# Attention outputs split at the end of their value products and kept in DRAM as two halves, in a hybrid attention and convolution trunk

## The chip, the cores and the metric

The kernel runs on one core of a Trainium2 chip. The metric is the device time of one execution in microseconds (us): the median of three runs of the kernel before is 903.31 us (902.05 to 904.63). The engines are TensorE (PE, its weight loads PEld), VectorE (DVE), ScalarE (ACT), GpSimd (POOL) and SyncE (SP), which issues most DMAs. Each engine takes its own instructions strictly in its order and waits where an operand is not there.

## The reference

1024 tokens of width 1024 pass two layers, each a pre-RMSNorm, a mixer and a residual; a last RMSNorm follows. All is float32. Layer 0 is latent attention with 8 heads, layer 1 a gated Conformer convolution. What the change touches is the end of the attention:

```
s = where(mask, (q @ k.T) * scale, -inf)       # causal, 8 heads, q and k 128 + 64 wide
p = softmax(s)
o = p @ v                                      # 128 wide for each head
out = (concat_heads(o) * silu(gate)) @ w_out   # 1024 x 1024
```

## The kernel before

Float32 products are made of three matmuls of halves: a value x is kept as a high half (x rounded to the matmul's type, a ScalarE copy) and a low half (x minus the high half, a VectorE subtraction), and `mm3` (lines 137 to 140) adds high x high, high x low and low x high in PSUM. Activations lie transposed, channels on the 128 partitions and tokens along the row; a chunk c is 512 of the 1024 tokens.

The attention runs over the heads h = 0 to 7. For head h, `score(h, i)` makes the scores S_i of the 128 queries of block i (five matmuls for each 512 keys, PSUM tile S, two buffers), adds the mask, takes the maximum (VectorE), the exponential (ScalarE, which frees the S buffer) and scales the probabilities P_i (GpSimd). `attend(h, c)` transposes the probabilities of four blocks piece by piece (T, TensorE), evacuates each piece as a high half pth (ScalarE, line 594) and a low half ptl (VectorE, line 595), each from a ring of four SBUF buffers, and adds the value products po (`mm3`). At its end the gating, line 599, writes og. For 15 of the 16 attends og is stored in DRAM as it is (`ogS`, line 602), 14 times on SyncE's queue and for (7,1) on GpSimd's. The attend (7,0) splits its og directly into the tiles of the output projection (`split_og`, lines 617 and 618).

attend(h,0) is called after S_5 of head h, attend(h,1) after S_1 of head h+1. `proj(h+1)`, which makes the next head's queries and keys (pj, qh, ql, kh, kl) and for every second head the values (pv, vh, vl), is called after S_3 of head h, `split_early` after S_6 and others. The calls do not set the final order: a scheduler puts each engine's instructions in an order when the kernel is built, and buffers that are reused carry waits. In what follows (h,c) is an attend, and the end of an attend is the place of its last value matmul.

`load_og` (lines 620 to 624) brings an og back: one load into the low half's place, then a ScalarE copy into the high half and a VectorE subtraction. The seven of chunk 0 are loaded while head 7 is at work, the eight of chunk 1 in the output projection, `o_tile`, whose weights are loaded (wr_o) and split as they are needed, from the same queue.

Of the kernel before, what the change touches and what calls it, by code (L numbers as in the profile page):

```python
# [9 lines left out]
F32 = mybir.dt.float32  # L10
F32R = mybir.dt.float32r
# [7 lines left out]
P = 128  # L19
# [3 lines left out]
NH = 8  # L23
CK = 31
NTAP = 16
CH = 512
# [38 lines left out]
def hybrid_body(ctx, tc, xT, xP, pos, cols, w1a, w1b, wqr, wqk, wv, wo, wc, we, out):  # L65
    nc = tc.nc
    v, s, g, pe, sp = nc.vector, nc.scalar, nc.gpsimd, nc.tensor, nc.sync
# [23 lines left out]
    ropeS = [[tc.dram_tile([P, T], F32, name=f"ropeS{k}{p_}") for p_ in range(2)]  # L91
             for k in range(4)]
    gateS = [tc.dram_tile([P, T], F32, name=f"gateS{h}") for h in range(NH)]
    ogS = [[tc.dram_tile([P, CH], F32, name=f"ogS{h}{c}") for c in range(2)] for h in range(NH)]

    early_eng = [v]

# [39 lines left out]
    def mm3(ps, wh, wl, xh, xl, start, stop):  # L137
        pe.matmul(ps, wh, xh, start=start, stop=False)  # L138
        pe.matmul(ps, wh, xl, start=False, stop=False)  # L139
        pe.matmul(ps, wl, xh, start=False, stop=stop)  # L140
# [64 lines left out]
    def halves(ap):  # L205
        return ap.rearrange("p (b n) -> p b n", b=2)

    def sl(k, n=P):
        return slice(k * n, (k + 1) * n)
# [56 lines left out]
    def load_a(k, many):  # L266


        raw = wp.tile([P, 1024], F32, tag="wraw", name=f"wr_a{k}")
        hi = wp.tile([P, 1024], F32R, tag="w", bufs=5, name=f"wh_a{k}")  # L270
        lo = wp.tile([P, 1024], F32R, tag="w", bufs=5, name=f"wl_a{k}")
        n = 384 * many
        sp.dma_start(raw[:, :n], w1a[:, 384 * k : 384 * k + n])
        if k == 0:
            v.tensor_copy(hi[:, :n], raw[:, :n])
        else:
            s.activation(hi[:, :n], raw[:, :n], AF.Copy)
        r3, h3, l3 = (t_[:, :n].rearrange("p (a n) -> p a n", n=384) for t_ in (raw, hi, lo))
        v.tensor_tensor(h3[:, :, 320:], r3[:, :, 320:], h3[:, :, 320:].bitcast(F32), ALU.subtract)
        v.tensor_tensor(l3[:, :, :256], r3[:, :, :256], h3[:, :, :256].bitcast(F32), ALU.subtract)  # L280
        return hi, lo

    for k in range(KD):
# [4 lines left out]
        if k == 0 or k % 2 == 1:  # L288
            first, many = k, 1 if k in (0, KD - 1) else 2
            pair = load_a(k, many)  # L290
# [196 lines left out]
    b1 = es_b.enter_context(tc.tile_pool(name="b1", bufs=1, reuse_waits="tile"))  # L487
# [92 lines left out]
    def attend(h, c, dst=None):  # L580
        vh, vl = vpair[h // 2]
        vs = sl(h % 2)
        gt = heads[h][5]
        po = psA_p.tile([P, CH], F32, tag="acc", name=f"po{h}{c}")
        nj = 4 * (c + 1)
        for j in range(nj):
            il0 = max(0, j - 4 * c)
            pt = psT_p.tile([P, CH], F32, tag="T", name=f"T{h}{c}{j}")
            for il in range(il0, 4):
                pe.transpose(pt[:, sl(il)], probs[h, 4 * c + il][:, sl(j)], ident)  # L590
            hi = b1.tile([P, CH], F32R, tag="pth", bufs=4, name=f"pth{h}{c}{j}")
            lo = b1.tile([P, CH], F32R, tag="ptl", bufs=4, name=f"ptl{h}{c}{j}")
            n0 = il0 * P
            s.activation(hi[:, n0:], pt[:, n0:], AF.Copy)  # L594
            v.tensor_tensor(lo[:, n0:], pt[:, n0:], hi[:, n0:].bitcast(F32), ALU.subtract)  # L595
            mm3(po[:, n0:], vh[:, j, vs], vl[:, j, vs], hi[:, n0:], lo[:, n0:],
                j == 0, j == nj - 1)
        og = b1.tile([P, CH], F32, tag="og", bufs=2, name=f"og{h}{c}")
        v.tensor_tensor(halves(og), po.rearrange("p (n b) -> p b n", b=2),
                        gt[:, sl(c, CH)].rearrange("p (n b) -> p b n", b=2), ALU.mult)  # L600
        if dst is None:
            (g if (h, c) == (NH - 1, 1) else sp).dma_start(ogS[h][c], og)
        else:
            split_og(og, dst)

    def act_tile(grp, nm):
        if grp == "A":
            both = long_tile([P, 2, CH], F32R, f"a_{nm}")
        elif grp == "B":
            both = mix_tile([P, 2, CH], F32R, f"a_{nm}")  # L610
        else:
            both = act.tile([P, 2, CH], F32R, tag="act", name=f"a_{nm}")
        return both[:, 0, :], both[:, 1, :]

    def split_og(raw, pair):
        hi, lo = pair
        s.activation(hi, raw, AF.Copy)
        v.tensor_tensor(lo, raw, hi.bitcast(F32), ALU.subtract)

    def load_og(grp, h, c):  # L620
        pair = act_tile(grp, f"og{c}{h}")
        sp.dma_start(pair[1].bitcast(F32), ogS[h][c])
        split_og(pair[1].bitcast(F32), pair)
        return pair

    ogt = {}
# [2 lines left out]
    for h in range(NH):  # L629
        for i in range(8):  # L630
            score(h, i)
            if i == 1 and pending is not None:
                attend(*pending)
                pending = None
            if i == 3 and h + 1 < NH:
                proj(h + 1)
            if i == 4 and h < 2:
                split_early(wc[22 + h], f"cg{6 + h}")
            if i == 6:
                split_early(we[h], f"e{h}")  # L640
            if i == 5:
                if h < NH - 1:
                    attend(h, 0)
                else:
                    ogt[0] = [load_og("A", h_, 0) for h_ in range(NH - 1)]
                    ogt[0].append(act_tile("A", f"og0{h}"))
                    attend(h, 0, ogt[0][h])
        pending = (h, 1)
# [95 lines left out]
    def pk_tile(nm):  # L744
        return dp.tile([P, CH], F32, tag="pk", bufs=3, name=nm)

    ogt[1] = [load_og("B", h, 1) for h in range(NH)]

    ctx.enter_context(tc.manual_schedule(engines={mybir.EngineType.PE}))
# [411 lines left out]
```

## Time and profile before

| | us |
|---|---|
| runs, median (range) | 903.31 (902.05 to 904.63) |
| the profiled execution, its own time | 903.44 |
| its span | 901.7 |
| attention, from about 180 to 452: length | 272.00 |
| output projection, from about 452 to 524: length | 72.00 |

The profiled execution's time is 1.7 us longer than its span, which begins with the first and ends with the last instruction. The mean granted TensorE clock is 0.996 of full speed. In a row of the timeline the first number is the start in us from the span's start, the second the duration; a bracket says how long the engine sat idle before the row and what ended that. A matmul's duration includes the time that it takes to pass the pipeline, so that successive starts, not durations, tell the pace.

### The profile page before, as it was taken

To read this page: it belongs to the slowest core of one execution; us is meant where nothing else is said; L and a number is where in the kernel's file an instruction comes from. 1 tells how busy PE (TensorE), PEld (TensorE's weight loads), DVE (VectorE), ACT (ScalarE), POOL (GpSimd) and SP (SyncE) were. 2 spreads that over 40 slices of the span, in tenths; PEclk is the share of its full clock that TensorE was granted. 3 is DMA by queue.
4 is the path that set the end of the run, shared out by engine and by line. 5 is a ranking of instruction groups with operands and counts; after the bars stand their busy time and mean duration, and the time that the engine had idled before them with its cause. 6 is when DMAs were issued, how large, how long until landed. Compare 5 with 4: busy or idle time off the path is not lost.

```text
span 901.7 us, 12318 instructions
## 1 busy us (share of the span) xinstructions
PE 888.1 (98%) x4408; PEld 739.4 (82%) x4408; DVE 656.6 (73%) x1123; ACT 503.1 (56%) x838; POOL 346.9 (38%) x296
## 2 busy tenths in 40 slices
PE   9999999999999999999999999999999999999996
PEld 7888887888988988988788888888888887878996
DVE  7688857556656566686465868999999998687544
ACT  8535355255655554574444457766566773678732
POOL 0000000142532421642212259999999993000034
PEclk9999999999999999999999999999999999999998
DMA  7325635572422331651274411111113223136714
GB/s 270 117 71 171 230 131 188 193 228 85 141 92 81 121 116 40 219 178 33 77 264 125 163 48 54 47 51 38 47 48 110 95 80 113 50 138 196 259 61 144
DMA packets 39836, 110.69 MB, mean 123 GB/s; under 512 B 5280, under 2 KB 8352, under 8 KB 39776
## 3 DMA queue, kind: packets, MB, share of 16 engines
q1 hardware_dynamic: 39408, 109.27, 36.5%
q8 instruction: 34, 0.56, 0.3%
q10 hardware_dynamic: 288, 0.39, 0.1%
q14 instruction: 26, 0.21, 0.1%
q0 software_dynamic: 80, 0.26, 0.1%
HBM read 83.93 MB, written 24.92 MB: 121 GB/s over the span
## 4 chain that ended last, share of the span: by engine, by line
PE 69%; POOL 15%; issue 6%; DVE 5%; ACT 2%; DMA 2%; SPq 0%; POOLq 0%; DVEq 0%; ACTq 0%
POOL dcv L850 13%; PE ps_b L138 5%; PE ps_b L140 5%; PE ps_b L139 5%; PE T L590 3%; PE o L139 3%; PE o L140 3%; PE o L138 3%; PE e L138 3%; PE e L140 3%; PE e L139 3%; PE po L139 2%; PE S L564 2%; PE S L567 2%; PE po L140 2%
## 5 line engine op out<-in xcount | busy, mean ns | idle before, releaser
L850 POOL TENSOR_TENSOR dcv<-dcv,pkb 128x512 f32<-128x512 f32 (+1 forms) x126 | 159.2, 1266 | 7.5
L849 ACT ACTIVATE pkb<-u,taps 128x512 f32<-128x512 f32 (+1 forms) x126 | 83.9, 674 | 56.8 <-POOL dcv L850 53.6
L577 POOL TENSOR_SCALAR P<-P,st 128x128 f32<-128x128 f32 (+3 forms) x64 | 47.7, 747 | 125.9 <-DVE st L576 124.1
L861 DVE SCALAR_TENSOR_TENSOR av<-u,taps,av 128x512 f32<-128x512 f32 (+1 forms) x135 | 91.6, 688 | 1.6 <-ACT av L855 1.5
L863 DVE SCALAR_TENSOR_TENSOR cv<-su,gsum,cv 128x512 f32<-128x512 f32 (+1 forms) x117 | 80.6, 689 | 0.5
L107 POOL TENSOR_TENSOR wl_qk<-wr_qk,wh_qk 128x640 fp32r<-128x640 f32 x8 | 12.6, 1571 | 170.4 <-DMA ropeS<-rh 164.3
L594 ACT ACTIVATE pth<-T 128x512 fp32r<-128x512 f32 (+1 forms) x96 | 46.0, 491 | 55.3 <-PE T L590 54.2
L138 PE MATMUL ps_b<-xgh,wh_b 128*128 128x512 f32 x176 | 69.9, 397 | 0.0
L140 PE MATMUL ps_b<-xgh,wl_b 128*128 128x512 f32 x176 | 69.6, 395 | 0.0
L139 PE MATMUL ps_b<-xgl,wh_b 128*128 128x512 f32 x176 | 69.6, 395 | 0.0
L595 DVE TENSOR_TENSOR ptl<-T,pth 128x512 fp32r<-128x512 f32 (+1 forms) x96 | 52.0, 552 | 22.2 <-ACT pth L594 22.0
L1040 POOL TENSOR_TENSOR x<-x,rbe 128x512 f32<-128x512 f32 (+1 forms) x16 | 16.2, 1046 | 125.3 <-DMA rbe<-rowe 120.1
L138 PE MATMUL e<-a_y,wh_e 128*128 128x256 f32 (+1 forms) x192 | 61.7, 322 | 0.0
L140 PE MATMUL e<-a_y,wl_e 128*128 128x256 f32 (+1 forms) x192 | 61.5, 320 | 0.0
L139 PE MATMUL e<-a_y,wh_e 128*128 128x256 f32 (+1 forms) x192 | 61.4, 320 | 0.0
L574 ACT ACTIVATE P<-S,st 128x128 f32<-128x128 f32 (+3 forms) x64 | 47.4, 742 | 23.3 <-DVE st L572 18.4
L138 PE MATMUL cg<-a_h,wh_cg 128*128 128x512 f32 x128 | 51.7, 404 | 0.0
L138 PE MATMUL o<-a_og,wh_o 128*128 128x512 f32 x128 | 50.9, 399 | 0.0
L140 PE MATMUL o<-a_og,wl_o 128*128 128x512 f32 x128 | 50.9, 397 | 0.0
L138 PE MATMUL cb<-a_h,wh_cb 128*128 128x512 f32 x128 | 50.8, 397 | 0.0
L138 PE MATMUL ca<-a_h,wh_ca 128*128 128x512 f32 x128 | 50.8, 397 | 0.0
L572 DVE TENSOR_REDUCE st<-S 128x1 f32<-128x128 f32 (+3 forms) x64 | 48.3, 754 | 3.5
(321 smaller groups left out, 2625.0 us busy)
## 6 DMA issues: line engine op xcount, KB each, us to landing
wr_o<-in_wo_dram SPq DMA_DIRECT2D x16, 512.0 KB, 4.4
wr_e<-in_we_dram SPq DMA_DIRECT2D x14, 512.0 KB, 4.4
wl_e<-loSe SPq DMA_DIRECT2D x14, 512.0 KB, 4.1
wr_b<-in_w1b_dram SPq DMA_DIRECT2D x11, 512.0 KB, 4.1
sr_cg<-in_wc_dram SPq DMA_DIRECT2D x8, 512.0 KB, 4.2
loScg<-sl_cg SPq DMA_DIRECT2D x8, 512.0 KB, 2.9
gateS<-gt SPq DMA_DIRECT2D x8, 512.0 KB, 4.5
rq<-ropeS SPq DMA_DIRECT2D x32, 128.0 KB, 2.8
```

The costliest lines, as they stand in the source:

```text
L138: pe.matmul(ps, wh, xh, start=start, stop=False)
L139: pe.matmul(ps, wh, xl, start=False, stop=False)
L140: pe.matmul(ps, wl, xh, start=False, stop=stop)
L572: v.tensor_reduce(st[:, 0:1], ps[:, off : off + nk], AX.X, ALU.max, negate=True)
L574: s.activation(pr[:, :nk], ps[:, off : off + nk], AF.Exp, bias=st[:, 0:1], accum_out=st[:, 1:2])
L577: g.tensor_scalar(pr[:, :nk], pr[:, :nk], st[:, 2:3], 1.0, ALU.mult, ALU.mult)
L594: s.activation(hi[:, n0:], pt[:, n0:], AF.Copy)
L595: v.tensor_tensor(lo[:, n0:], pt[:, n0:], hi[:, n0:].bitcast(F32), ALU.subtract)
L849: s.activation(pk, lag(src, i), AF.Copy, scale=tap(of, i))
L850: g.tensor_tensor(acc, acc, pk, ALU.add)
L861: v.scalar_tensor_tensor(a_, lag(E, i), tap(dwe, i), a_, ALU.mult, ALU.add)
L863: v.scalar_tensor_tensor(c_, lag(su, i), tap(gsum, i), c_, ALU.mult, ALU.add)
```

## The change

`attend` splits og where it makes it, into two tiles that it takes from the rings pth and ptl (four buffers each), and stores both in two DRAM tiles. `load_og` loads both halves and splits nothing. 15 ScalarE and 15 VectorE operations move from the loads to the ends of the attends; 15 stores and 15 loads of 256 KB are added. The lines behind the first hunk are one higher in the kernel after, and up to seven higher behind the second.

```diff
-    ogS = [[tc.dram_tile([P, CH], F32, name=f"ogS{h}{c}") for c in range(2)] for h in range(NH)]
+    ogS = [[[tc.dram_tile([P, CH], F32, name=f"ogS{h}{c}{a}") for a in range(2)]
+            for c in range(2)] for h in range(NH)]
...
         if dst is None:
-            (g if (h, c) == (NH - 1, 1) else sp).dma_start(ogS[h][c], og)
+            pair = [b1.tile([P, CH], F32R, tag=t_, bufs=4, name=f"og{t_}{h}{c}")
+                    for t_ in ("pth", "ptl")]
+            split_og(og, pair)
+            for a in range(2):
+                (g if (h, c) == (NH - 1, 1) else sp).dma_start(
+                    ogS[h][c][a], pair[a].bitcast(F32))
         else:
             split_og(og, dst)
...
     def load_og(grp, h, c):
         pair = act_tile(grp, f"og{c}{h}")
-        sp.dma_start(pair[1].bitcast(F32), ogS[h][c])
-        split_og(pair[1].bitcast(F32), pair)
+        for a in range(2):
+            sp.dma_start(pair[a].bitcast(F32), ogS[h][c][a])
         return pair
```

The orders of the engines differ in the attention only. In the rows below a name's number is the program's own and differs between the two kernels. The first place is the end of attend (1,0). ScalarE before (pth_2319, pth_2331 and pth_2343 belong to attend (0,1), the next):

```order
L120 ACTIVATE sh_e_2594<-sr_e_2592 128x512 x2
L105 ACTIVATE wh_qk_2775<-wr_qk_2773 128x640
L594 ACTIVATE pth_2319<-T_2314 128x512
L594 ACTIVATE pth_2331<-T_2326 128x512
L594 ACTIVATE pth_2343<-T_2338 128x512
L105 ACTIVATE wh_v_2827<-wr_v_2825 128x512
```

ScalarE after (ogpth is the high half of (1,0), pth_2350 and pth_2362 belong to (0,1)):

```order
L121 ACTIVATE sh_e_2635<-sr_e_2633 128x512 x2
L106 ACTIVATE wh_qk_2821<-wr_qk_2819 128x640
L623 ACTIVATE ogpth_2266<-og_2264 128x512
L595 ACTIVATE pth_2350<-T_2345 128x512
L595 ACTIVATE pth_2362<-T_2357 128x512
L106 ACTIVATE wh_v_2873<-wr_v_2871 128x512
```

The high half stands ahead of the next attend's evacuations, and the third of these has moved behind the split of a weight, wh_v. TensorE at the same place after, from the last value matmul of (1,0), po_2221, to the first of (0,1), po_2344:

```order
L141 MATMUL po_2221<-pth_2257,vl_1582 128x128
L569 MATMUL S_5_2546<-krl,rq_2048 128x512
L565 MATMUL S_5_2546<-kh_2063,qh_2061 128x256
L566 MATMUL S_5_2546<-kl_2064,qh_2061 128x256
L567 MATMUL S_5_2546<-kh_2063,ql_2062 128x256
L568 MATMUL S_5_2546<-krh,rq_2048 128x256
L569 MATMUL S_5_2546<-krl,rq_2048 128x256
L139 MATMUL po_2344<-pth_2350,vh_1581 128x512
L139 MATMUL pj_2486<-qnh_137,wh_qk_2478 128x512
```

Before, po's first matmul of the next attend followed the last of this one directly. The second place is the end of attend (1,1), where the next head's scores begin; (3,1) and (5,1) read alike. TensorE before, from the last two matmuls of S_7 of that head (S_7_2602) on:

```order
L567 MATMUL S_7_2602<-krh,rq_2022 128x512
L568 MATMUL S_7_2602<-krl,rq_2022 128x512
L138 MATMUL po_2313<-pth_2388,vh_1565 128x256
L139 MATMUL po_2313<-ptl_2389,vh_1565 128x256
L140 MATMUL po_2313<-pth_2388,vl_1566 128x256
L590 MATMUL T_2529<-ident,P_0_2296 128x128
L590 MATMUL T_2529<-ident,P_1_2309 128x128
L590 MATMUL T_2529<-ident,P_2_2416 128x128
L590 MATMUL T_2529<-ident,P_3_2429 128x128
L564 MATMUL S_0_2620<-kh_2448,qh_2446 128x128
L138 MATMUL pj_2483<-kvh_127,wh_qk_2442 128x512
L139 MATMUL pj_2483<-kvl_129,wh_qk_2442 128x512
```

TensorE after, at the last matmuls of S_7 (here S_7_2643):

```order
L567 MATMUL S_7_2643<-kh_2063,ql_2062 128x512
L139 MATMUL pj_2519<-kvh_143,wh_qk_2478 128x512
L140 MATMUL pj_2519<-kvl_145,wh_qk_2478 128x512
L141 MATMUL pj_2519<-kvh_143,wl_qk_2480 128x512
L139 MATMUL pj_2519<-kvh_144,wh_qk_2478 128x512
L140 MATMUL pj_2519<-kvl_146,wh_qk_2478 128x512
L141 MATMUL pj_2519<-kvh_144,wl_qk_2480 128x512
L568 MATMUL S_7_2643<-krh,rq_2048 128x512
L569 MATMUL S_7_2643<-krl,rq_2048 128x512
L139 MATMUL po_2344<-pth_2419,vh_1581 128x256
L140 MATMUL po_2344<-ptl_2420,vh_1581 128x256
```

The key projection pj, six matmuls of 512 columns, has moved from behind S_7 and the first of S_0 to ahead of the last two of S_7; S_0, the last three value matmuls and S_1 follow it in both. The third place is the end of attend (2,1), the head's first scores. ScalarE before, from the exponential P_0 of head 3 on:

```order
L574 ACTIVATE P_0_3030,st_0_3027<-S_0_3021,st_0_3027 128x128
L543 ACTIVATE vh_2831<-pv_2848 128x512
L594 ACTIVATE pth_2965<-T_2963 128x128
L574 ACTIVATE P_1_3043,st_1_3040<-S_1_3034,st_1_3040 128x256
L120 ACTIVATE sh_e_3328<-sr_e_3326 128x512 x2
L543 ACTIVATE vh_2831<-pv_2863 128x512
L574 ACTIVATE P_2_3150,st_2_3147<-S_2_3141,st_2_3147 128x384
```

ScalarE after, from the same exponential on:

```order
L575 ACTIVATE P_0_3081,st_0_3078<-S_0_3072,st_0_3078 128x128
L544 ACTIVATE vh_2877<-pv_2879 128x512
L544 ACTIVATE vh_2877<-pv_2894 128x512
L121 ACTIVATE sh_e_3389<-sr_e_3387 128x512 x2
L595 ACTIVATE pth_3002<-T_2999 128x256
L575 ACTIVATE P_1_3094,st_1_3091<-S_1_3085,st_1_3091 128x256
L544 ACTIVATE vh_2877<-pv_2909 128x512
L575 ACTIVATE P_2_3206,st_2_3203<-S_2_3197,st_2_3203 128x384
```

The early split sh_e has moved from behind P_1 to ahead of it.

## Rows read from the trace of the kernel before

**Rows 1.** The page: busy time and share of each engine.

```profile
PE 888.1 (98%) x4408; PEld 739.4 (82%) x4408; DVE 656.6 (73%) x1123; ACT 503.1 (56%) x838; POOL 346.9 (38%) x296
```

**Rows 2.** Windows: stretch, length, busy (instructions) of PE, PEld, DVE, ACT, POOL; clock; DMA; GB/s.

```profile
180.00:452.00 272.00, 269.35 (x1556) 233.25 (x1555) 170.69 (x366) 147.67 (x318) 97.92 (x99) 1.00 0.37 118
452.00:524.00 72.00, 72.00 (x310) 57.95 (x309) 48.60 (x63) 30.63 (x43) 16.14 (x14) 1.00 0.53 175
...
460.00:465.00 5.00, 5.00 (x23) 4.04 (x22) 3.36 (x3) 3.17 (x5) 2.40 (x1) 1.00 1.05 394
```

**Rows 3.** Waits of PEld, 180 to 452: us, times, longest.

```profile
PEld S L564 <- ACT P L574: 3.1, 7, 1.1
PEld po L139 <- DVE ptl L595: 1.9, 4, 0.8
PEld po L138 <- ACT pth L594: 1.0, 3, 0.4
```

**Rows 4.** Timeline, TensorE at its pace (five of 512, three of 256 columns).

```profile
314.87 0.39 PE L564 MATMUL S<-kh,qh 128*128 128x512 f32 x1
...
316.03 0.28 PE L564 MATMUL S<-kh,qh 128*128 128x256 f32 x1
...
316.39 0.28 PE L567 MATMUL S<-krh,rq 128*128 128x256 f32 x1
```

**Rows 5.** Timeline, the end of attend (1,0).

```profile
251.86 1.12 ACT L594 ACTIVATE pth<-T 128x512 fp32r<-128x512 f32 x2 [0.50 <-PE po L140]
...
252.65 0.28 PE L140 MATMUL po<-pth,vl 128*128 128x128 f32 x1
...
252.76 0.44 PE L138 MATMUL po<-pth,vh 128*128 128x512 f32 x1
...
253.10 0.68 DVE L599 TENSOR_TENSOR og<-po,gateB 128x512 f32<-128x512 f32 x1
253.24 0.19 PEld L139 LDWEIGHTS po<-ptl,vh 128*128 128x128 f32 x1 [0.34 <-DVE ptl L595]
```

**Rows 6.** Timeline, the end of attend (1,1), from the last matmul of S_7.

```profile
268.82 0.39 PE L568 MATMUL S<-krl,rq 128*128 128x512 f32 x1
...
269.25 0.30 DVE L571 TENSOR_TENSOR S<-S,mask 128x128 f32<-128x128 f32 x1
...
269.65 1.22 DVE L572 TENSOR_REDUCE st<-S 128x1 f32<-128x1024 f32 x1
...
270.91 1.12 ACT L574 ACTIVATE P<-S,st 128x1024 f32<-128x1024 f32 x1 [0.21 <-DVE st L572]
...
272.63 1.12 POOL L577 TENSOR_SCALAR P<-P,st 128x1024 f32<-128x1024 f32 x1
...
274.17 0.39 ACT L574 ACTIVATE P<-S,st 128x128 f32<-128x128 f32 x1
...
274.70 0.19 PEld L564 LDWEIGHTS S<-kh,qh 128*128 128x128 f32 x1 [0.43 <-ACT P L574]
```

**Rows 7.** Timeline, the end of attend (5,1).

```profile
398.77 1.10 ACT L574 ACTIVATE P<-S,st 128x1024 f32<-128x1024 f32 x1
...
400.02 0.19 PEld L564 LDWEIGHTS S<-kh,qh 128*128 128x128 f32 x1 [1.14 <-ACT P L574]
```

**Rows 8.** Timeline, the end of attend (2,1): S_3, and the early split.

```profile
308.19 0.48 PE L564 MATMUL S<-kh,qh 128*128 128x512 f32 x1
...
309.14 1.15 ACT L120 ACTIVATE sh_e<-sr_e 128x512 fp32r<-128x512 f32 x2 [2.29 <-DMA sr_e<-in_we_dram]
```

**Rows 9.** The stores of line 602, from issue to landing.

```profile
DMA to landing us min/median/max: 2.0/3.4/7.1
```

**Rows 10.** Line 618 (count: min/median/max ns), and VectorE and GpSimd around 461.6.

```profile
L618 DVE TENSOR_TENSOR a_og<-a_og x15: 673/683/2822, 388.0 to 469.2; 128x512 fp32r<-128x512 f32 x15
...
461.64 4.03 DVE L618 TENSOR_TENSOR a_og<-a_og 128x512 fp32r<-128x512 f32 x3 [2.75 <-ACT a_og L617]
...
461.51 2.40 POOL L107 TENSOR_TENSOR wl_o<-wr_o,wh_o 128x1024 fp32r<-128x1024 f32 x1 [9.53 <-PE o L140]
```

## The prediction, made before the changed kernel ran

> **What bounds the kernel now.** I read the page first: TensorE is busy 98% of the span and every other engine at most 73% [rows 1]. Then the windows, one for each stretch that the change touches: in the attention TensorE works 269.35 of 272.00 us at full granted clock, in the output projection 72.00 of 72.00 [rows 2]. So time is TensorE's instruction stream, which the change leaves at the same number of matmuls, plus the moments in which that stream stands still. The view of waits says where it stands still in the attention: 3.1 us for the exponentials that free a score buffer, 1.9 and 1.0 us for the low and high transposed probabilities [rows 3]. That is 6.0 us, and at most that much can be won there. With so little idle time nothing absorbs a new stall: each us that the stream stands longer is a us of the kernel. The question is what the moved instructions stand in front of.
>
> TensorE's pace comes from starts in the timeline: five 512-column matmuls take 1.16 us (0.23 each), three of 256 columns 0.36 (0.12 each) [rows 4]; one of 128 columns, and a transpose, takes 0.11 [rows 5].
>
> **Part 1: the splits leave the load.** 15 ScalarE splits of some 0.56 us (each of two like it [rows 5]) and 15 VectorE splits of 0.68 [rows 10] go from the loads. Eight pairs lie in the output projection, where TensorE never waits [rows 2]: worth 0. Seven lie in head 7's attention; of the 6.0 us of waits [rows 3] 1.9 stand at three ends of attends named below, and of the remaining 4.1 I let 0.5 go with these seven pairs (bounds 0 and 4.1; nearer to 0, since seven pairs are spread beside dozens of other ScalarE operations).
>
> **Part 2: the splits come to the ends of the attends, and into the ring of the transposed probabilities.** This is the costly part. The halves use the tags pth and ptl, so ScalarE's high half takes its turn in that ring: in the new order every attend's high half stands ahead of the next attend's first two evacuations (the first two ScalarE pieces of the section on the change). Before, those stood ahead of the gating. The first value product of the next attend therefore now waits for this chain, counted from the start of the last value matmul: 0.28 until its result is there, 0.04 and the gating 0.68 [rows 5], 0.04 and the high half, behind which the next ScalarE operation starts 0.56 later (two in 1.12), that evacuation 0.56 to 0.60 and 0.05 to TensorE: 2.2 us. What TensorE has to do in these 2.2 us is read from its order.
>
> At the end of attend (1,0) it is (the TensorE piece that follows) one 128-column, one 512-column and five 256-column matmuls: 0.11 + 0.23 + 0.60 = 0.94 us. Stall 1.26; before it stood 0.34 there [rows 5]. Net **+0.9**. At (2,0) to (5,0), (2,1), (4,1) and (6,1) the same count gives 2.3 us and more, so nothing; at (6,0) the low half comes 0.1 late: **+0.1**. At (7,0) the direct split is as before.
>
> At (1,1), (3,1) and (5,1) more is late, since the six matmuls of the key projection that stood behind the last S_7 matmul before now stand ahead of it (the next two TensorE pieces). I set the last value matmul at 0. From the order at the pace above, the last S_7 matmul starts at -1.82 (0.23, three of 0.12, four transposes of 0.11, five and two of 0.11), S_1 of the next head at 0.36 ahead of which only the last value matmul and three transposes stand (before, 1.4 us more work lay between the two), the first value product at 1.03, S_2 at 1.27. Against that stands the chain of S_7: 0.43 to the mask, 0.30 for it, a low half of the keys that VectorE now does in between, 0.68 (the duration of its other 512-column operations), and 1.26 from the reduction to the exponential [rows 6], so P_7 starts at 0.85, and S_1 starts 1.25 after that [rows 7]: at 2.10, a stall of 1.74. ScalarE's high half follows the exponential at 1.95, the first evacuation 0.56 later, the first product at 3.15. The second evacuation (three quarters of 0.56, so 0.42) lets P_0 start at 3.48, and S_2 starts 0.53 behind P_0's start [rows 6]: at 4.01 instead of 1.27, 2.7 in all; I take **2.6**, since the reduction may run a little ahead. Before, 0.43 and 1.14 us were lost at (1,1) and (5,1) [rows 6, 7] and next to nothing at (3,1). So 7.8 - 1.6 = **+6.2**. Bounds: 1.0 each if only the chain of the gating counts (2.2 against 1.03), 3.3 each if the low half is late as well.
>
> **Part 3: a waiting instruction that others queue behind.** At (2,1) ScalarE's order puts the early split sh_e ahead of P_1's exponential (the last two pieces). sh_e waited 2.29 us for its load and began at 309.14, and S_3 began at 308.19 [rows 8], unhurt because P_1 was already done. Now S_3 needs sh_e (1.15), an evacuation and P_1 (about 0.5 each with the release) first: about 311.2, where TensorE's order would reach it at about 308.8. That is +2.4 with this landing, and nothing with one 2.4 us earlier. I take **+1.5**, nearer to the row.
>
> **Part 4: the DMAs.** 15 more stores, 15 more loads of 256 KB. Stores land 2.0 to 7.1 us after their issue, 3.4 in the median [rows 9], and the half lies in one of four slots until then. The fifth allocation of a ring comes some 3 to 6 us later in an attend, so mostly 0 (up to 1 us each time a late landing holds a slot). In the output projection the DMA engines are full at 394 GB/s [rows 2]; eight more loads of 256 KB are 8 x 0.66 = 5.3 us, but GpSimd's split of a weight had waited 9.53 us for TensorE to free its buffer [rows 10], so the weights wait for TensorE there and not the reverse: 0, at the worst 2.
>
> **Sum.** -0.5 + 0.9 + 0.1 + 6.2 + 1.5 = +8.2 us against the profiled execution's own 903.44: 911.6. That execution lies 0.13 above the median of the runs, so the forecast is **911.5 us**, slower.
>
> **A rule that makes it worse.** VectorE's low half of a_og took 0.68 us in the median and 2.82 once, when GpSimd's 2.40 us split of a weight began 0.13 us before three of them [rows 10]. The Trainium skill says in "SBUF — State Buffer", section "SBUF: two separate sides", that a VectorE operation with two SBUF inputs and a GpSimd operation exclude each other for the whole instruction; this case's trace agrees (2.82 against 0.68). By that rule the moved low half, which comes right behind the reciprocal that starts GpSimd's scaling of P_7, would at the three ends wait up to that scaling's 1.12 us [rows 6], the low transposed half behind it would be some 0.6 late, and the sum would be +10.
>
> **Rivals.**
> - Low half against GpSimd, at (1,1), (3,1), (5,1). For it: the 2.82 of [rows 10]. Against: if the low half starts first, GpSimd waits, and nobody waits for that at once. Price 3 x 0.6 = 1.8: 913.3.
> - Stores hold the ring. For it: landings up to 7.1 us [rows 9], about 13 evacuations stand in a slot that a store must leave. Against: the median 3.4. If a third of them wait 1 us on the way to TensorE: +4, 915.5.
> - Everything covered: no change, 903.4. It holds if ScalarE and VectorE run far enough ahead that the high half is done early. Against: the chain begins with the last value matmul itself, so nothing can run ahead of it.
> - Faster: the load-side splits are what delays head 7. The wait of 1.14 us at 400.02 [rows 7] stands just behind six of them, P_7's exponential late in ScalarE's queue; if that stall and two thirds of the remaining 1.9 + 1.0 us [rows 3] go, and the ends of the attends cost nothing, 900.4. It decides only if the stalls of part 2 are below 1 us together.
> - The change might not do what it says, the halves being kept whole; the order shows two stores, so I give that no chance.
>
> **How the numbers follow.** Forecast 0.52; GpSimd 0.15; stores 0.13; covered 0.14; faster 0.06. The range holds the forecast from the low bounds (3 x 1.0 - 1.6 + 0.9 + 0 - 0.5 = +1.8) to the high ones with GpSimd or the stores (+12.5). I cut it to 905.0 and 916.0: below lie the covered and the faster case, 0.17 or so, above a little. About 2.7 us (0.3%) is what a measurement of this kernel can tell from no change; slower by more: the forecast and the two costlier cases, less a little for low bounds, 0.79; faster 0.06; the same 0.15.
>
> **What would show it.** In the profile after, TensorE's busy time in the attention stays near 269 us while the stretch grows by some 8; the waits of S for P grow from 3.1 to about 7 us, those of po for pth from 1.0 to 3 or more, in three places about 2.6 us each; the output projection stays full. If the three ends show under 1 us each, the sum is wrong in part 2; if S_3 at (2,1) does not wait, in part 3; if pth waits for a DMA, the stores were mis-sized.

## The result, and the profile after

The kernel after takes 919.19 us in the median (917.81 to 920.82), the kernel before 903.13 beside it: the ratio is 1.0171, 95% interval 1.0159 to 1.0182. Slower was the right side, but 16.1 us is twice the 8.2 forecast and lies outside the range, which ended at 916.0. The profiled execution took 918.18 us, 14.7 more than that of before.

The windows, for the stretches that answer to [rows 2] (stretch, length, busy time and instructions of PE, PEld, DVE, ACT, POOL, granted clock, DMA share, GB/s):

```profile
180.00:466.00 286.00, 275.93 (x1555) 237.16 (x1554) 178.66 (x373) 150.83 (x324) 97.50 (x98) 0.98 0.41 131
466.00:540.00 74.00, 73.33 (x315) 58.70 (x314) 45.28 (x57) 28.31 (x38) 20.51 (x16) 1.00 0.59 205
```

Nearly all of it is in the attention: about the same matmuls (1555 against 1556) need 286 us instead of 272. TensorE's idle time there has grown from 2.65 to 10.07 us, much as forecast. But its busy time, which the prediction kept near 269, has grown too, from 269.35 to 275.93, and the granted clock of the stretch is 0.98 instead of 1.00. That is the part that the prediction did not have. In the output projection TensorE stands still for 0.67 us. The waits, beside [rows 3]; the last line is of the output projection:

```profile
PEld S L565 <- ACT P L575: 6.9, 7, 1.7
PEld po L139 <- ACT pth L595: 4.4, 9, 1.3
PEld po L140 <- DVE ptl L596: 3.0, 6, 0.7
PEld pv L539 <- PE T L591: 1.6, 2, 0.8
...
PEld o L141 <- DVE wl_o L108: 1.1, 1, 1.1
```

S now waits 6.9 us for the exponentials (3.1 before; "about 7" forecast) and po 4.4 us for the high halves (1.0; "3 or more"). The last two rows are new and were not forecast. The end of attend (1,1) in the timeline, which answers to [rows 6]:

```profile
273.26 0.52 PE L591 MATMUL T<-ident,P 128*128 128x128 f32 x3
...
273.94 1.11 ACT L575 ACTIVATE P<-S,st 128x1024 f32<-128x1024 f32 x1 [0.95 <-DVE st L573]
...
275.05 0.62 ACT L623 ACTIVATE ogpth<-og 128x512 fp32r<-128x512 f32 x1
...
275.20 0.19 PEld L565 LDWEIGHTS S<-kh,qh 128*128 128x128 f32 x1 [1.66 <-ACT P L575]
...
275.44 1.12 POOL L578 TENSOR_SCALAR P<-P,st 128x1024 f32<-128x1024 f32 x1 [2.98 <-DVE st L577]
...
275.70 1.40 DVE L624 TENSOR_TENSOR ogptl<-og,ogpth 128x512 fp32r<-128x512 f32 x1 [0.36 <-ACT ogpth L623]
...
276.21 0.80 PE L139 MATMUL po<-pth,vh 128*128 128x512 f32 x1
...
276.94 0.69 PE L565 MATMUL S<-kh,qh 128*128 128x384 f32 x1
```

The wait for S_1 is the forecast one: its weight load stood 1.66 us (1.74 forecast), and by the matmuls' starts the first value product and S_2 came another 0.17 and 0.49 late, 2.3 in all (2.6 forecast). Behind the wait the rows look different: a 512-column matmul lasts 0.80 us and one of 384 columns 0.69, where [rows 6] have 0.39 for 512 columns. The windows of single microseconds tell why (columns as above):

```profile
274.00:275.00 1.00, 0.00 (x0) 0.00 (x0) 0.84 (x3) 1.00 (x2) 0.00 (x0) 1.00 1.00 169
275.00:276.00 1.00, 0.80 (x5) 0.80 (x5) 0.46 (x2) 1.00 (x4) 0.56 (x1) 0.79 0.67 254
276.00:277.00 1.00, 1.00 (x4) 0.39 (x3) 1.00 (x1) 0.89 (x4) 0.56 (x1) 0.50 1.01 319
277.00:278.00 1.00, 1.00 (x4) 1.00 (x4) 1.00 (x4) 0.00 (x0) 0.00 (x0) 0.50 0.89 311
278.00:279.00 1.00, 1.00 (x4) 1.00 (x4) 0.82 (x4) 0.27 (x1) 0.07 (x1) 0.50 0.93 358
279.00:280.00 1.00, 1.00 (x7) 0.87 (x7) 0.87 (x3) 0.33 (x3) 0.30 (x1) 1.00 0.31 119
```

Some 0.4 us after TensorE resumes, its granted clock falls to 0.50, that is 1.2 instead of 2.4 GHz, and comes back at 279: four matmuls in each us instead of seven. At (3,1) and (5,1) it falls 1.4 us after TensorE resumes, for as long. The three ends look alike in windows of 10 us:

```profile
270.00:280.00 10.00, 8.58 (x44) 7.29 (x43) 7.46 (x17) 5.24 (x14) 3.46 (x4) 0.83 0.60 188
340.00:350.00 10.00, 8.21 (x39) 6.90 (x39) 7.78 (x19) 4.84 (x14) 2.56 (x4) 0.83 0.58 190
410.00:420.00 10.00, 8.87 (x45) 7.80 (x46) 6.80 (x19) 4.88 (x15) 2.83 (x5) 0.83 0.50 184
```

0.83 in 10 us is 1.7 us of TensorE's time lost in each, part of it under the waits that still follow. No other window of 10 us between 200 and 490 us shows less than 1.00, and between 180 and 524 none of before does.

### The profile page after: what moved, and what is told of

It is laid out like the page before. It is cut to its first block, busy times and chain, and to the rows that moved or that the text cites. A ratio compares the mean times of both kernels' runs of the same rounds, so it can differ in the third digit from the quotient of the medians.

```text
span 916.3 us, 12393 instructions
## 1 busy us (share of the span) xinstructions
PE 895.3 (98%) x4408; PEld 744.2 (81%) x4408; DVE 657.4 (72%) x1123; ACT 503.4 (55%) x838; POOL 349.9 (38%) x297
## 4 chain that ended last, share of the span: by engine, by line
PE 66%; POOL 13%; DVE 7%; issue 6%; ACT 3%; DMA 3%; SPq 1%; POOLq 0%; DVEq 0%; ACTq 0%
POOL dcv L856 12%; PE ps_b L139 5%; PE ps_b L141 4%; PE ps_b L140 4%; PE e L139 3%; PE e L141 3%; PE e L140 3%; PE o L141 3%; PE o L140 3%; PE o L139 3%; PE T L591 3%; PE po L140 2%; DVE cv L869 2%; PE S L565 2%; PE po L141 2%
## 5 line engine op out<-in xcount | busy, mean ns | idle before, releaser
L108 POOL TENSOR_TENSOR wl_qk<-wr_qk,wh_qk 128x640 fp32r<-128x640 f32 x8 | 12.5, 1568 | 172.5 <-DMA ropeS<-rh 164.3
L108 POOL TENSOR_TENSOR wl_o<-wr_o,wh_o 128x1024 fp32r<-128x1024 f32 x9 | 24.4, 2707 | 72.9 <-PE o L140 29.6
L140 PE MATMUL o<-a_og,wh_o 128*128 128x512 f32 x128 | 50.9, 398 | 0.0
L139 PE MATMUL o<-a_og,wh_o 128*128 128x512 f32 x128 | 50.9, 399 | 0.0
```

The source lines that it names most:

```text
L108: (eng or early_eng[0]).tensor_tensor(lo[:, :n], raw[:, :n], hi[:, :n].bitcast(F32), ALU.subtract)
```

## The experiments

Theory A is that of the prediction with the clock added: the order that the ring forces on ScalarE, and with it on TensorE, makes TensorE wait at the ends of (1,1), (3,1) and (5,1), and the fallen clock costs another 1.4 us or so behind each. Its rivals are B, the doubled stores and loads, and C, the splits at the ends wherever they lie.

**The halves in buffers of their own.**

```diff
-        og = b1.tile([P, CH], F32, tag="og", bufs=2, name=f"og{h}{c}")
+        og_r = b1.tile([P, CH], F32R, tag="og", bufs=1, name=f"og{h}{c}")
+        og = og_r.bitcast(F32)
...
-            pair = [b1.tile([P, CH], F32R, tag=t_, bufs=4, name=f"og{t_}{h}{c}")
-                    for t_ in ("pth", "ptl")]
+            pair = [b1.tile([P, CH], F32R, tag="ogh", bufs=1, name=f"ogh{h}{c}"), og_r]
```

> Edit of the kernel after: the high half lies in a buffer of its own (one), the low half is written over og (one buffer instead of two), so the halves no longer take turns in the rings pth and ptl. Work, stores and loads are those of the kernel after. Theory A (the ring's order makes TensorE wait at the ends of (1,1), (3,1), (5,1), 1.7 us for S_1 and some 2.4 us in all each, and the clock that falls to 1.2 GHz behind each wait costs about 1.4 us more): three times 3.8 us and the 1.3 us at (1,0) go, about 919 - 12 = 907 us, the granted clock at 1.00 in all of the attention. Rival B (the doubled stores and loads cost the time): 919 as before, since every DMA is still there. Rival C (the moved splits themselves are too much for ScalarE and VectorE at the ends of attends, wherever their buffers lie): 914 or more.

904.96 us, ratio to before 1.0015 (1.0006 to 1.0024). With all 15 stores, 15 loads and 30 moved splits, 14 of the 16 us are gone by taking the halves out of the ring. The order, which the scheduler made anew, explains it: the next attend's first two evacuations stand ahead of the high half again, and the key projection behind S_7. The end of (1,1) in its timeline, and the window around it, show one short wait of po for a low half, none for an exponential, and a clock of 1.00:

```profile
274.26 0.65 ACT L623 ACTIVATE ogh<-og 128x512 fp32r<-128x512 f32 x1
...
275.12 0.44 PE L140 MATMUL po<-ptl,vh 128*128 128x384 f32 x1 [0.51 <-DVE ptl L596]
```

```profile
270.00:280.00 10.00, 9.49 (x60) 8.25 (x60) 8.47 (x22) 7.23 (x18) 3.80 (x5) 1.00 0.56 192
```

B and C fall as main causes: the transfers and the splits at the ends are all still there.

**Filler for TensorE in the three waits.**

```diff
-            for il in range(il0, 4):
-                pe.transpose(pt[:, sl(il)], probs[h, 4 * c + il][:, sl(j)], ident)
+            for rep in range(5 if (c, j) == (0, 1) and h in (2, 4, 6) else 1):
+                for il in range(il0, 4):
+                    pe.transpose(pt[:, sl(il)], probs[h, 4 * c + il][:, sl(j)], ident)
```

> Edit of the kernel after: the three transposes that TensorE does last before its wait for S_1 at the ends of (1,1), (3,1) and (5,1) are done five times over (12 more transposes, some 1.3 us of work, in each of the three places, same result); the wait chain is as it was. Theory A: TensorE would have stood still for these 1.3 us; the wait for S_1 falls from 1.7 to some 0.4 us, the clock stays at 2.4 GHz, and the kernel is faster with 36 more instructions, by 3 times 1.4 us, about 915. Rival (the clock fell for another reason than the wait, say the stretch's work): granted clock 0.83 in the same 10 us windows again and 919 or more, since the filler is only more work.

913.85 us, 5.3 faster than the kernel after with 36 instructions more (ratio to before 1.0109, 1.0092 to 1.0126, against 1.0171). The mean granted clocks of its four executions are 0.997, 0.996, 0.997, 0.996; those of the kernel after are 0.991, 0.992, 0.990, 0.994. The rows at (1,1), and the window:

```profile
273.04 1.83 PE L592 MATMUL T<-ident,P 128*128 128x128 f32 x15
273.72 1.11 ACT L575 ACTIVATE P<-S,st 128x1024 f32<-128x1024 f32 x1 [0.95 <-DVE st L573]
...
274.97 0.19 PEld L565 LDWEIGHTS S<-kh,qh 128*128 128x128 f32 x1 [0.34 <-ACT P L575]
```

```profile
270.00:280.00 10.00, 9.48 (x60) 7.99 (x59) 7.86 (x19) 6.12 (x15) 3.71 (x5) 1.00 0.62 190
```

The exponential comes as late as before the edit and S_1 starts behind it as late; the only thing that changed is that TensorE worked while it waited. So the three falls of the clock hang on the wait, and they cost about 4 to 5 us in the kernel (5.3 between the medians, 4.0 by the table further down). In the one profiled execution, 916.37 us, the slowest of the four, S_3 at (2,1) waits as part 3 of the prediction said:

```profile
312.13 1.15 ACT L121 ACTIVATE sh_e<-sr_e 128x512 fp32r<-128x512 f32 x2 [3.57 <-DMA sr_e<-in_we_dram]
...
313.45 0.46 ACT L575 ACTIVATE P<-S,st 128x256 f32<-128x256 f32 x1
...
314.06 0.50 PE L565 MATMUL S<-kh,qh 128*128 128x512 f32 x1 [1.07 <-ACT P L575]
```

The early split waits 3.57 us for its load, P_1 stands behind it, and S_3 behind P_1. The same happens at (4,1) there, and at both places in the profile of the run with the old way below. The profile of the kernel after has no such wait: there the early split waits 2.33 us for its load, and S_3 does not stand behind it. It hangs on when the load lands.

**Waits put into the output projection of before.**

```diff
+    HOLD = {(0, 3): (512,), (0, 5): (512, 512), (0, 7): (512, 512, 256), (1, 2): (512, 512, 512),
+            (1, 4): (512, 512, 512, 256), (1, 6): (512, 512, 512, 512)}
...
+        def hold():
+            for n_ in HOLD[c, m]:
+                t_ = wh[:, 384 : 384 + n_]
+                s.activation(t_, t_.bitcast(F32), AF.Copy)
+        if (c, m) in HOLD:
+            mid = (4, hold)
```

> Edit of the kernel before: in six tiles of the output projection, some 11 us apart, ScalarE copies a part of the weights' high half onto itself between the fourth and the fifth of the eight steps, one to four copies in a row, so that TensorE, otherwise never idle there, waits about 0.6, 1.2, 1.5, 1.7, 2.1 and 2.4 us. Theory A: behind the waits of 1.7 us and more the granted clock falls to half for about 3 us (another 1.5 us lost by each of those), behind those of 1.2 us and less it stays. Rival (it is not the wait but what else happens at the ends of attends, as DMAs or transposes): the clock stays at 1.00 behind all six.

One execution only, 927.0 us. The waits came out longer than meant, since other work of ScalarE stood between: 0.71, 4.77, 1.82, 3.67, 2.42 and 2.63 us by the matmuls' starts. Two of the first matmuls behind a wait, and then the windows of 2 us behind these two:

```profile
483.78 0.50 PE L138 MATMUL o<-a_og,wh_o 128*128 128x512 f32 x1 [1.65 <-ACT wh_o L687]
...
521.01 0.79 PE L138 MATMUL o<-a_og,wh_o 128*128 128x512 f32 x1 [2.25 <-ACT wh_o L687]
```

```profile
484.00:486.00 2.00, 2.00 (x10) 1.59 (x10) 0.00 (x0) 0.00 (x0) 0.00 (x0) 1.00 0.00 0
...
522.00:524.00 2.00, 2.00 (x6) 1.58 (x5) 0.00 (x0) 0.00 (x0) 0.00 (x0) 0.50 0.00 0
```

With all four waits of 2.42 us and more the clock fell to half, and in the windows shown no DMA ran and neither VectorE, ScalarE nor GpSimd worked; behind 1.82 and 0.71 it did not fall. It fell for some three us with 2.42 and 2.63, and for some seven with 3.67 and 4.77; in three of the four it was down before TensorE resumed. So a wait alone does it. The expectation that 1.7 would do it always was wrong.

**The three outputs the old way.**

```diff
+    OLD = ((1, 1), (3, 1), (5, 1))
...
-        if dst is None:
+        if dst is None and (h, c) in OLD:
+            sp.dma_start(ogS[h][c][0], og)
+        elif dst is None:
...
+        if (h, c) in OLD:
+            sp.dma_start(pair[1].bitcast(F32), ogS[h][c][0])
+            split_og(pair[1].bitcast(F32), pair)
+            return pair
```

> Edit of the kernel after: the three outputs (1,1), (3,1) and (5,1) go the way of before (stored whole, loaded whole, split at the load); the other twelve are as in the kernel after. Theory A: three times (2.4 us of waits + 1.4 us of clock) = 11.4 us go, less the 1.6 us of waits that the kernel before has there: about 909 us, with 1.00 granted clock in the attention. Rival B (stores and loads): 12 of 15 doubled transfers stay, so 916. Rival C (splits at any end): 12 of 15 stay: 916.

914.24 us (ratio 1.0117, 1.0102 to 1.0132): 5 us faster than the kernel after, not 10. The wait for S_1 is still there:

```profile
274.91 0.39 PE L565 MATMUL S<-kh,qh 128*128 128x256 f32 x1 [1.48 <-ACT P L575]
```

1.66 us by the starts, as in the kernel after, though no output is split here. Its cause is the key projection ahead of the last two S_7 matmuls, and this order is made elsewhere. In this execution the granted clock is 1.00 in the windows of 10 us around all three ends, behind the same 1.66 us. The mean clocks of the four executions are 0.997, 0.994, 0.997, 0.995; 0.994 lies below all executions of the kernel before (0.995 to 0.997), so it fell in that one at least.

**The DMAs alone.** This is the kernel before with the two DRAM tiles of the change. The splits are left out altogether: both places of the pair get the unsplit output.

```diff
-            (g if (h, c) == (NH - 1, 1) else sp).dma_start(ogS[h][c], og)
+            for a in range(2):
+                (g if (h, c) == (NH - 1, 1) else sp).dma_start(ogS[h][c][a], og)
...
-        sp.dma_start(pair[1].bitcast(F32), ogS[h][c])
-        split_og(pair[1].bitcast(F32), pair)
+        for a in range(2):
+            sp.dma_start(pair[a].bitcast(F32), ogS[h][c][a])
```

> Edit of the kernel before: each of the 15 outputs is stored twice and loaded twice, into both places of its pair, and the split at the load is left out (so the halves are not made at all). The orders of TensorE and of the other engines' work stay those of before. This is the change's DMAs alone, without the moved splits. Theory A (order of ScalarE, then the clock): 903 within 2 us, the granted clock 1.00 in the attention, no wait of S or po longer than the 1.1 us of before. Rival B (doubled stores and loads): most of the change's 16 us, so 911 or more.

910.2 us (ratio 1.0065, 1.0047 to 1.0083). Neither theory had that. Little of it is in the attention, where the longest wait of S for P has grown from 1.1 to 1.8 us and the clock stays at 1.00; the windows and the waits of the output projection show where it is:

```profile
180.00:450.00 270.00, 266.33 (x1541) 230.85 (x1539) 163.87 (x354) 141.81 (x308) 96.62 (x98) 1.00 0.42 138
450.00:532.00 82.00, 77.30 (x325) 61.19 (x325) 44.79 (x61) 28.58 (x39) 21.51 (x17) 0.98 0.54 188
```

```profile
PEld o L139 <- ACT wh_o L106: 2.9, 1, 2.9
PEld o L141 <- DVE wl_o L108: 2.8, 2, 2.0
```

Weights are late there, once with a fall of the clock behind it. SyncE's rows offer a reason for the first: this kernel issues all 16 loads (455.69 to 468.92) and then the next weight; in the kernel after, a weight stands ahead of them, so that SyncE's order differs outside the attention too, unlike what the section on the change says:

```profile
455.69 13.23 SPq L625 DMA_DIRECT2D a_og<-ogS  x16
469.27 9.87 SPq L104 DMA_DIRECT2D wr_o<-in_wo_dram  x4
```

```profile
471.13 0.33 SPq L104 DMA_DIRECT2D wr_o<-in_wo_dram  x1
471.50 11.56 SPq L629 DMA_DIRECT2D a_og<-ogS  x16
```

So late weights, which the prediction gave 0 to 2 us, can cost 5 or so of these 6; in the kernel after they cost 0.8. That the one weight more ahead of the loads makes the difference is read from the orders and was not tried; and the low half of a weight is late by 2.1 us in the run with only the three outputs below too, which has three loads more and not fifteen.

**Only the three outputs in the ring, and only (1,0), (3,0), (5,0).** Both take the edit of the run with the old way and change the list (the second names (1, 0), (3, 0) and (5, 0)):

```diff
+    OLD = [(h_, c_) for h_ in range(NH) for c_ in range(2) if (h_, c_) not in ((1, 1), (3, 1), (5, 1))]
```

> Edit of the kernel after: only the outputs (1,1), (3,1) and (5,1) are split at the end of the attend and go through the rings; the other twelve go the way of before. TensorE's order keeps the key projection behind S_7 there, as in the kernel before. Theory A as it stands now (two causes meet at these three ends: the high half ahead of the next attend's evacuations, and the key projection that the entries of (1,0), (3,0), (5,0) moved ahead of the last S_7): the high half alone makes the first value product wait about 1 us at each of the three ends, S_1 does not wait longer than before, and the clock stays at 1.00: 903.4 + 3 to 4 = about 907. Rival (the high half at these ends is the whole cause): about 914, with granted clock 0.83 in the three windows.

> Edit of the kernel after: only the outputs (1,0), (3,0) and (5,0) are split at the end of the attend and go through the rings; the other twelve go the way of before. TensorE's order has the key projection ahead of the last two S_7 matmuls in heads 1, 3 and 5, as in the kernel after, though no output there is split at its end. Theory A as it stands now: S_1 of the next head waits 1.7 us at the three ends (the chain of S_7 alone), 3 x 1.7 less the 1.6 us of before, 0.9 at (1,0): about 907 to 908; the granted clock stays at 1.00 if the waits of po and S_2 behind it are needed for its fall, as in the run with the old way at these ends. Rival (no output is split at these ends, so they behave as before): 904.

912.75 us (1.0078 to 1.0112) with the three, 911.69 (1.0067 to 1.0101) with (1,0), (3,0) and (5,0) alone. Both expectations were too low, though the mechanisms are there. With the three alone, at (1,1):

```profile
273.24 1.15 ACT L121 ACTIVATE sh_e<-sr_e 128x512 fp32r<-128x512 f32 x2
274.28 0.63 ACT L627 ACTIVATE ogpth<-og 128x512 fp32r<-128x512 f32 x1
274.80 0.97 ACT L597 ACTIVATE pth<-T 128x512 fp32r<-128x512 f32 x2
275.44 0.19 PEld L139 LDWEIGHTS po<-pth,vh 128*128 128x128 f32 x1 [1.78 <-ACT pth L597]
```

```profile
270.00:280.00 10.00, 8.20 (x43) 7.05 (x42) 6.70 (x17) 5.74 (x15) 3.21 (x4) 0.83 0.58 191
```

The key projection is behind S_7, S_1 is in time, and the first value product waits 1.73 us instead of the 1 expected, because an early split of 1.15 us stands ahead of the high half as well; the clock falls here too, but in this execution not at the two other ends, where the value products wait 0.8 and 1.0 us, (3,1), and a score tile 1.1, (5,1). With (1,0), (3,0), (5,0) alone the key projection is moved, and S_1 waits at an end where nothing is split (first row). At (1,0), where the halves enter, no score matmuls lie ahead of the next attend's first value product in this kernel, and it waits for the whole chain of part 2 (second row), 2.26 us from the last value matmul's start at 253.10, where the prediction has 2.2; the clock stays at 1.00 behind both:

```profile
276.70 0.39 PE L565 MATMUL S<-kh,qh 128*128 128x256 f32 x1 [1.49 <-ACT P L575]
...
255.36 0.19 PEld L139 LDWEIGHTS po<-pth,vh 128*128 128x128 f32 x1 [2.13 <-ACT pth L597]
```

So two orders, each made by entries in the ring, are each enough for a wait of 1.7 us at such an end: the high half ahead of the next attend's evacuations, and the key projection ahead of S_7, which follows from the entry of the attend before. The kernel after has both. How its 16 us divide between them does not follow from the 9 and 8 us of these two: they are costs of whole kernels, and both kernels also wait for the low half of a weight in the output projection (2.1 and 1.7 us) and for halves of queries and keys (2.1 and 1.5 us, 0.4 before), for reasons that were not tried.

**One chunk in buffers of its own.** The first expectation is for chunk 0, the second for chunk 1; the edit is that of the run with the old way, on the kernel with buffers of their own and with a condition on c in place of the list.

> Edit of the run with the halves in buffers of their own: only the outputs of chunk 0, (0,0) to (6,0), are split at the end of the attend; those of chunk 1 go the way of before. Theory A (no ring, so no chain ahead of the next attend): within 2 us of before, and it shows whether the seven splits that leave head 7's attention are worth the 0.5 us that the prediction gave them: 902 to 903 if they are, 904 to 905 if the doubled loads that stand ahead of the weights in head 7 cost as much as in the run with all halves.

> Edit of the run with the halves in buffers of their own: only the outputs of chunk 1, (0,1) to (7,1), are split at the end of the attend; those of chunk 0 go the way of before. Theory A: within 2 us of before, 903 to 905; nothing can be won, since the splits leave the output projection, where TensorE does not wait. Rival B (the doubled loads of the output projection make a weight late, as in the run with the doubled DMAs alone): 906 to 910, with a wait of o for a weight of some 2 us.

Chunk 0: 903.5 us, ratio 1.0002 (0.9994 to 1.0011). Moving the seven splits from head 7's attention to the ends of their attends is worth nothing on balance that can be measured. Chunk 1: 908.96 (1.0050 to 1.0074), but not by rival B's wait in the output projection; the largest place is in head 7, a wait for a high half. ScalarE's row and TensorE's:

```profile
414.64 0.63 ACT L625 ACTIVATE a_og<-a_og 128x512 fp32r<-128x512 f32 x1 [3.64 <-DMA a_og<-ogS]
...
415.81 0.19 PEld L139 LDWEIGHTS po<-pth,vh 128*128 128x128 f32 x1 [1.71 <-ACT pth L595]
```

```profile
410.00:420.00 10.00, 8.24 (x38) 6.69 (x37) 5.61 (x11) 2.98 (x6) 1.50 (x2) 0.85 0.18 54
```

ScalarE waits 3.64 us for the load of an output that is split at the load, and the next high half stands behind that split in its order: a stall without any entry in the ring, of the kind of part 3. The clock falls again in this window. No kernel tried is faster than before.

## Why the prediction was wrong

Its direction and its mechanism stood; the sum lacked a term, the slower clock behind the waits. Where the numbers below have no row, they are sums of successive matmuls' starts in the profile after, less the pace of [rows 4, 5].

| step of the prediction | forecast | measured |
|---|---|---|
| part 2, waits at (1,1), (3,1), (5,1) | 7.8 less 1.6 | 2.3 + 2.5 + 2.5 = 7.2, less 1.6 |
| the clock behind these waits | not in the sum | +4.0 |
| part 2, (1,0) | +0.9 | +1.0 |
| part 2, (6,0) | +0.1 | +0.9 |
| part 3, (2,1) | +1.5 | +0.9, and +0.9 at (4,1) |
| part 1, head 7 | -0.5 | +1.0 |
| part 4, output projection | 0 | +0.8 |
| behind the output projection | not in the sum | -0.4 |
| sum | +8.2 | +14.7 in the profiled execution |

- **The failed step is the sum of part 2.** It added up waits and took TensorE's pace of [rows 4] for the time behind them. The profile after has a granted clock of 0.50 for about three microseconds behind each of the three; the filler run shows that the wait is what brings it. That run's median of 913.85, with the clock kept up, lies inside the range: the missing term is what put the result outside. The prediction could have seen a warning only indirectly: the longest wait of before was 1.14 us [rows 7] and its clock never fell in the attention, so no row showed what 1.7 us would do.
- **The two chains of part 2 were right**, to a tenth of a us at (1,0) and within 0.3 at the three ends. (S_1's place of 0.36 in that working should be 0.44 by its own pace, one value matmul and three transposes of 0.11; little hangs on it.) What the prediction left out of its reading is that they are independent: taking the three outputs out of the ring leaves the wait for S_1.
- **Part 3** named a real wait, which the profiles of the filler run (1.07 us idle for P) and of the run with the old way show, and the profile after does not. There, the values' matmuls wait instead, for VectorE's low half of the values, at (2,1) and in the same way at (4,1); why these are later was not tried.
- **Part 1** had the wrong sign: head 7 lost a us more in waits of a few tenths, and taking the splits out of its loads won nothing on balance (chunk 0 in buffers of its own). The row from which the "faster" rival argued does not bear it: between the six splits and the 1.14 us wait [rows 7] ScalarE was idle for 1.17 and 1.06 us, and with chunk 0 in buffers of its own the same wait is still 1.07 us, with those six gone. In another order such a split can delay head 7, as the chunk 1 run shows. **(6,0)** lost 0.9 us to a weight, not to the high half: ScalarE waits 2.17 us for the weight's load, with the evacuations behind it in its order:

```profile
394.13 1.06 ACT L106 ACTIVATE wh_o<-wr_o 128x1024 fp32r<-128x1024 f32 x1 [2.17 <-DMA wr_o<-in_wo_dram]
395.10 1.07 ACT L595 ACTIVATE pth<-T 128x512 fp32r<-128x512 f32 x2
```
- **GpSimd's rival.** The moved low half took 1.40 us at 275.70 instead of 0.68, beginning inside GpSimd's scaling (275.44, 1.12 us) and ending 0.54 behind it; the 2.82 of [rows 10] ended 0.55 behind GpSimd's operation. The trace agrees with the Trainium skill's rule ("SBUF — State Buffer", "SBUF: two separate sides") that one of the two is shut out until the other's instruction is done. No row of TensorE waits for it there, as S_2 and the slow clock came first, so the price of 0.6 us each is not seen in the kernel after. With the clock kept up, in the filler run, the low product waits 0.43 us at each of the three ends.
- **The stores' rival** exists, but off the path. In the profile after two high halves and three low ones wait for a store to leave their slot, 1.7 us on each of the two engines, all for the last piece of an attend, the longest this one:

```profile
244.90 0.28 ACT L595 ACTIVATE pth<-T 128x128 fp32r<-128x128 f32 x1 [1.49 <-DMA ogS<-ogpth]
```

  No row of TensorE waits behind any of them.
- **The range** ended at 916.0, which is its high end of +12.5 us. The upper bounds of its own parts add up to more, 0 + 0.9 + 0.1 + 8.3 + 2.4 + 2 = +13.7 us, none of them stood for the clock, and the small terms of part 1, (6,0) and part 4 came out higher than taken.

The runs' median lies a us above the profiled execution; the executions of the kernel after differ by 3 us and in their mean clock (0.990 to 0.994), so the clock's share is not the same in each.

## What to carry to other kernels

A buffer borrowed from a ring costs its place in the ring's order: what is put in at a late moment holds up everything that takes the next slots, on every engine that fills them, and a scheduler may move other work in answer. Read from the new order what each engine now does ahead of the first instruction that the bottleneck needs next; one extra buffer (here one shared out of the room of another) gave back 14 of 16 us. And when a forecast gives TensorE a wait longer than any in the trace, price the slower clock behind it as a term of its own.

## What the runs showed of the hardware that was not expected

TensorE's granted clock fell to 0.50 (1.2 GHz) for about three us behind waits of 1.66 us (three times in the kernel after), 1.73 (three outputs in the ring), 1.72 (chunk 1 in buffers of its own), 2.42 and 2.63 (the waits put in) and 2.6 (the DMAs alone), and for about seven with 3.67 and 4.77. It stayed at 1.00 behind waits as long or longer: 1.66 three times where the output was split at the load, 1.82 (put in), and 1.66 twice and 2.13 with (1,0), (3,0), (5,0) alone. The mean clocks of single executions vary as well. So the length of a wait alone does not decide it between 1.6 and 2.4 us, and what else does was not found; that TensorE's own filler work keeps the clock up was shown, in all four executions of that run (mean clocks 0.996 and 0.997).
